# Two orders on ScalarE in a hybrid attention block: the mix gates' Sigmoids, and the first casts of the MLP's block sums

## The chip, the cores and the metric

One core of one Trainium2 chip. The metric is the device time of one execution in microseconds; the time of a kernel is the median of its runs. The engines are TensorE (PE; its weight loads are PEld), VectorE (DVE), ScalarE (ACT), GpSimd (POOL) and SyncE (SP, which here only issues DMAs).

## The reference

One layer with batch 1, sequence 1024, width 1024, all in float32. Cut to what matters:

```python
h = rms_norm(x, g_pre_mix)
proj = h @ w_in                       # q, k, v of both branches, and two gates of 1024 columns
gates = sigmoid(proj[..., c1:]);  gate_sb, gate_diff = split(gates, 2)
y_sb   = stick_breaking_attention(...)            # 8 heads of 64; sigmoids and a product along the keys
y_diff = differential_attention(...)              # 4 heads; two softmax maps, chunk-causal, T5 bias
y_diff = rms_norm(y_diff, w_subln) * (1 - lam_init)
merged = gate_sb * (y_sb @ w_sb_out) + gate_diff * (y_diff @ w_diff_out)
x = x + rms_norm(merged @ w_o, g_post_mix)
h = rms_norm(x, g_pre_mlp)
u = square(relu(h @ w_up))                        # 1024 -> 4096
x = x + rms_norm(u @ w_down, g_post_mlp)
```

## The kernel before

Every matrix product is made of three matmuls on split operands: an operand is cast to the matmul's type (`hi`, on ACT) and the rest is subtracted (`lo`, on DVE); the products are hi·hi, hi·lo and lo·hi. A cast followed by a subtraction is thus the commonest pair of instructions. Some of the gate projections and the whole MLP use a fast 2x2 block scheme with seven products in place of eight, on sums of blocks (T1 to T4 of the right operand, w1, w24, w32 of the left); the sums are formed on DVE or POOL.

The program is written in stages, and the Tile framework orders it (`schedule_with_timeline_sim=True`): it runs the whole program in a timing model and puts an instruction on its engine's list when the model has it ready, older work first. Each engine then works down its list in order, and waits at the head of it. The stages that matter here:

- *Attention* runs over eight units: four pairs of stick-breaking heads (`steps_sb`, Sigmoids on ACT), then four differential heads (`steps_diff`, Exps on ACT). A unit runs over four groups j of two query tiles in the order 3, 1, 2, 0. Its end, `finish_diff`, transposes the weights on PE (`tr_df`), splits them (`wth_df`, L298, and `wtl_df`), multiplies with v (`av_d`, L368 to L370), and for j = 1 and 0 normalises: a copy of `av_d` (L375), a Square, the split of it (`yp`, L379), a matmul with ones (`ss`, L382), then Ln (L385) and Exp (L386) on ACT, four DVE steps, and a split that is stored to DRAM as y. Between the steps of a unit the kernel fills PE with projections of the next unit and with gate products; beside the last unit these are `last_products` (L542 on PE: g_b, g_c, g_d; `split_pair` casts their weights at L596; page_v is a running sum).
- *One activation table at a time.* A manual dependency (`after`) keeps the differential Exps behind the last Sigmoid of the stick-breaking heads, and one table with both Ln and Exp is loaded there by hand. Any other table load is put in by the compiler ahead of an activation that the loaded table lacks.
- *The mix* follows. `load_gate` loads a gate from DRAM into a buffer that attention's score tiles also use (`big_s`, four of them), and takes the Sigmoid (L721). `half_mix` loads and splits a weight, calls `load_gate`, and makes a product of 24 matmuls (L755) from y into one of the four pairs of PSUM banks (acc, sc, tr, av). `merge` multiplies the banks with the gates (L766), adds the halves (L768) and splits the sum (L769, L770), which frees the banks and the gate buffers. Sixteen half products are made in all, two of them ahead.
- *The output projection* (`finish_tile`, L859) runs over eight row tiles, with norms; `store_h` transposes the MLP's input and stores it in blocks, and for the last two tiles copies it straight into `hraw`.
- *The MLP's entry*. `load_h` loads `hraw` back. Eight products (L981) of two pairs of weights are computed ahead with the blocks B11 and B21, which exist early; after B11 the bank is copied out (L1001, `p1s`), then B21 is added in the same bank and relu and square follow (L987, L988). Meanwhile DVE forms the block sums from `hraw` and `split` makes hi and lo of B22, T2, T1, T3 and T4 (L810 and L811), first for the 384 early columns, then for the last 128. Then `up_pair` runs over the sixteen pairs of weights.

Loads and most stores are issued by SP in list order.

Of the kernel before, what the change touches and what calls it, by code (L numbers as in the profile page):

```python
# [11 lines left out]
AF = mybir.ActivationFunctionType  # L12
# [30 lines left out]
def hybrid_block_kernel(  # L43
# [17 lines left out]
    nc = tc.nc  # L61
# [20 lines left out]
    def f32(ap):  # L82
        return ap.bitcast(F32)
# [71 lines left out]
    with ExitStack() as actx:  # L155
# [129 lines left out]
        def transposed(w, j, name):  # L285

            for g in range(j + 1):
                tr = tr_tile(f"tr_{name}_{g}")
                cols = [(2 * g, 0), (2 * g, 1)]
                cols += [(2 * g + 1, 0), (2 * g + 1, 1)] if g < j else [(2 * g + 1, 1)]  # L290
                for i, (kb, qi) in enumerate(cols):
                    nc.tensor.transpose(  # L292
                        tr[:, i * P:(i + 1) * P], w[qi][:, kb * P:(kb + 1) * P], ident
                    )
                n = len(cols) * P
                hi = pa.tile([P, HALF], F32R, tag="wt_hi", name=f"wth_{name}_{g}", bufs=2)
                lo = pa.tile([P, HALF], F32R, tag="wt_lo", name=f"wtl_{name}_{g}", bufs=2)
                nc.scalar.copy(hi[:, :n], tr[:, :n])  # L298
                nc.vector.tensor_tensor(lo[:, :n], tr[:, :n], f32(hi[:, :n]), op=ALU.subtract)  # L299
                yield 2 * g, slice(0, 256), hi[:, 0:256], lo[:, 0:256]  # L300
                if g < j:
                    yield 2 * g + 1, slice(0, 256), hi[:, 256:512], lo[:, 256:512]
                else:
                    yield 2 * g + 1, slice(P, 256), hi[:, 256:384], lo[:, 256:384]
# [4 lines left out]
        def pair_bank(key, j):  # L309

            if j > 1:
                banks[key, j % 2] = ps.tile([P, 2, 256], F32, tag="av", name=f"av_{key}_{j}", bufs=2)
            return banks[key, j % 2]

        def store_y(u, rows, j, yt):
            y_rows = y_dram[u][rows].rearrange("p l (h o c) -> p l h o c", h=2, o=2)
            for part in range(2):
                nc.sync.dma_start(out=y_rows[:, part, :, j % 2, :], in_=f32(yt[:, part]))
# [45 lines left out]
        def finish_diff(h, j, w, v):  # L364
            bank = pair_bank(f"d{h}", j)
            av = bank[:, j // 2, :]
            for kb, qc, hi, lo in transposed(w, j, f"df{h}_{j}"):
                nc.tensor.matmul(av[:, qc], v[:, kb, 0:P], hi, start=(kb == 0), stop=False)  # L368
                nc.tensor.matmul(av[:, qc], v[:, kb, 0:P], lo, start=False, stop=False)
                nc.tensor.matmul(av[:, qc], v[:, kb, P:2 * P], hi, start=False, stop=(kb == 2 * j + 1))  # L370
            if j > 1:
                return
            yt = pa.tile([P, 2, 256], F32, tag="part", name=f"y_{h}_{j}", bufs=2)
            sq, r = (pa.tile([P, 2, 256], F32, tag="small_s", name=f"{n}_{h}_{j}", bufs=4) for n in ("sq", "r"))
            nc.scalar.copy(yt, bank)  # L375

            nc.scalar.activation(sq, yt, AF.Square)
            both = pa.tile([P, 2, 2, 256], F32R, tag="yt", name=f"yp_{h}_{j}", bufs=1)
            nc.scalar.copy(both[:, 0], sq)  # L379
            nc.vector.tensor_tensor(both[:, 1], sq, f32(both[:, 0]), op=ALU.subtract)  # L380
            ss = ps.tile([P, 2, 256], F32, tag="av", name=f"ss_{h}_{j}", bufs=2)
            nc.tensor.matmul(ss, ones, both[:, 0], start=True, stop=False)  # L382
            nc.tensor.matmul(ss, ones, both[:, 1], start=False, stop=True)

            nc.scalar.activation(r, ss, AF.Ln, scale=1.0 / P, bias=eps_col)  # L385
            nc.scalar.activation(r, r, AF.Exp, scale=-0.5)  # L386
            nc.vector.scalar_tensor_tensor(sq, ss, P * EPS, r, op0=ALU.add, op1=ALU.mult)
            nc.vector.scalar_tensor_tensor(sq, sq, -0.5 / P, r, op0=ALU.mult, op1=ALU.mult)
            nc.vector.scalar_tensor_tensor(sq, sq, 1.5, r, op0=ALU.add, op1=ALU.mult)
            nc.vector.scalar_tensor_tensor(yt, yt, subln, sq, op0=ALU.mult, op1=ALU.mult)  # L390
            nc.scalar.copy(both[:, 0], yt)
            nc.vector.tensor_tensor(both[:, 1], yt, f32(both[:, 0]), op=ALU.subtract)
            store_y(N_SB + h, slice(0, P), j, both)

        def steps_diff(h, qs, kh, kl, v):
# [5 lines left out]
            for j in ORDER:  # L401
                w = []
                for qt in (2 * j, 2 * j + 1):
# [27 lines left out]
                    )  # L431
                    w.append(p1)
                yield 4 * j + 3, partial(finish_diff, h, j, w, v)

        last_sigmoid = [None]

        def after(ins, first):
            tc.add_manual_dep(
                ins.ins, first.ins.name,
                mybir.DependencyInfo(mybir.DependencyClass.NoSync, mybir.DependencyReason.DATA),  # L440
                reason="one activation table at a time",
            )
# [275 lines left out]
        def load_gate(b, i):  # L718
            g = pa.tile([P, S], F32, tag="big_s", name=f"g_{b}_{i}", bufs=4)
            nc.sync.dma_start(out=g, in_=gate_dram[i * NK + b])  # L720
            nc.scalar.activation(g, g, AF.Sigmoid)  # L721
            return g


# [68 lines left out]
    def pair_page(name, dt=F32R):  # L793
        return page(name, [P, 2, HALF], dt)
# [11 lines left out]
    def raw_tile(name, shape=None):  # L806
        return stream.tile(shape or [P, S], F32, tag="raw", name=f"raw_{name}")

    def split(hi, lo, raw):
        nc.scalar.copy(hi, raw)  # L810
        nc.vector.tensor_tensor(lo, raw, f32(hi), op=ALU.subtract)  # L811

    def bank(tag, name):
        return ps.tile([P, HALF], F32, tag=tag, name=name, bufs=2)
# [28 lines left out]
    def split_h(name, q, raw):  # L843
        split(*hb[name][q], raw)
# [106 lines left out]
    for t in range(NT):  # L951
# [12 lines left out]
        if t == 3:  # L964
            for name, j in (("B11", 0), ("B21", 1)):
                h_pages(name, big_pair)
                for q in range(2):
                    raw = raw_tile(f"h{name}{q}", [P, 2, HALF])
# [5 lines left out]
    def product(acc, a, b, first=True):  # L974

        a_hi, a_lo = a
        for k in range(4):
            ks = slice(k * P, (k + 1) * P)
            h_hi, h_lo = (x[:, k % 2, :] for x in hb[b][k // 2])
            for i, (st, mv) in enumerate(((a_hi, h_hi), (a_hi, h_lo), (a_lo, h_hi))):  # L980
                nc.tensor.matmul(  # L981
                    acc, st[:, ks], mv, start=(first and k == 0 and i == 0), stop=(k == 3 and i == 2),
                    skip_group_check=True,
                )

    def relu2(dst, src):
        nc.scalar.activation(dst, src, AF.Relu)  # L987
        nc.scalar.activation(dst, dst, AF.Square)  # L988

    def blocks(pages, i):  # L990
        return tuple(x[:, i * HALF:(i + 1) * HALF] for x in pages)
# [3 lines left out]
    p1s = [pair_page(f"p1_{i}", F32) for i in range(AHEAD // 2)]  # L995
    u11s = [pair_page(f"u11_{i}", F32) for i in range(AHEAD // 2)]
    for i in range(AHEAD // 2):
        accs = [bank(BANKS[i % 2], f"c11_{2 * i + e}") for e in range(2)]
        for e in range(2):
            product(accs[e], blocks(first_a[2 * i + e], 0), "B11")  # L1000
            nc.scalar.copy(p1s[i][:, e, :], accs[e])  # L1001
        for e in range(2):
            product(accs[e], blocks(first_a[2 * i + e], 1), "B21", first=False)
            relu2(u11s[i][:, e, :], accs[e])
            state.append((p1s[i][:, e, :], u11s[i][:, e, :]))
# [6 lines left out]
    for cs in (EARLY, LATE):  # L1012
        def split_part(name, q, raw):
            hi, lo = hb[name][q]
            split(hi[:, :, cs], lo[:, :, cs], raw)

        hs = [[hraw[j, c, q][:, :, cs] for j, c in ((0, 1), (0, 0), (1, 1), (1, 0))] for q in range(2)]
        for q, (b12, b11, b22, b21) in enumerate(hs):
            nc.vector.tensor_tensor(b11, b12, b11, op=ALU.subtract)
            split_part("B22", q, b22)  # L1020
            nc.vector.tensor_tensor(b12, b22, b12, op=ALU.subtract)
            nc.vector.tensor_tensor(b22, b22, b11, op=ALU.subtract)
            split_part("T2", q, b22)
        for q, (b12, b11, b22, b21) in enumerate(hs):
            split_part("T1", q, b11)
        for q, (b12, b11, b22, b21) in enumerate(hs):
            split_part("T3", q, b12)
        for q, (b12, b11, b22, b21) in enumerate(hs):
            nc.vector.tensor_tensor(b21, b21, b22, op=ALU.subtract)
            split_part("T4", q, b21)  # L1030
# [193 lines left out]
    for left, other in zip(STORED, ("B11", "T1", "T2", "T4", "T3", "B22", "B21")):  # L1224
        accs = [bank(BANKS[t], f"d{left}_{t}") for t in range(4)]
# [63 lines left out]
```

## Time and profile before

| what | value |
|---|---|
| median of 3 runs | 1462.94 us (1461.15 to 1464.65) |
| profiled execution | 1466.77 us |
| its span, first to last instruction | 1465.0 us |
| PE busy | 1432.6 us, 98% of the span |
| DVE, ACT, POOL busy | 1019.1, 759.3, 395.9 us |
| mean granted clock of PE | 0.995 |
| the 16 Sigmoids of L721 | 623.5 to 738.1 us from the start, 1.06 us each |
| the 8 Exps of L386 | 414.6 to 672.8 us |
| the 4 copies of L1001 | 844.1 to 863.0 us |

Rows of the profile are read so. In the order of time: start in us from the span's start, duration in us, engine, line of the kernel, operation, written tile <- read tiles, shape, and how many in a row; in brackets the idle time of the engine before it and what ended it (`<-DMA g<-gate_dram` is the DMA that wrote g). In the list of waits: who waited for whom, total us, times, longest. In a group: busy us, mean ns of one | idle us before them and what ended it. In a table by stretches: length, then busy us and count for each engine, then PE's granted clock, the share of the DMA engines and GB/s.

### The profile page before, as it was taken

How to read it: one execution, taken by the hardware profiler on the slowest of the kernel's cores; microseconds unless marked ns; L12 is line 12 of the kernel's file. 1: busy time of each engine (PE TensorE's matmuls, PEld its weight loads, DVE VectorE, ACT ScalarE, POOL GpSimd, SP SyncE). 2: the span in 40 equal slices, each digit the busy share in tenths (PEclk: the TensorE clock that was granted, in tenths of full speed). 3: DMA queues.
4: the chain of work that ended last, by engine and by line, in shares of the span. 5: the costliest groups of instructions: out<-in, count | busy, mean ns of one | idle time of the engine just before them, and what ended most of it. 6: DMA issues, size and time to landing. Idle time of an engine off the chain costs nothing.

```text
span 1465.0 us, 19999 instructions
## 1 busy us (share of the span) xinstructions
PE 1432.6 (98%) x7238; PEld 1213.6 (83%) x7238; DVE 1019.1 (70%) x1354; ACT 759.3 (52%) x1316; POOL 395.9 (27%) x393
## 2 busy tenths in 40 slices
PE   7999999999999999989999989999999999999997
PEld 6888998898889888768888877888888888888886
DVE  5477998898667768754756499766665669764783
ACT  5455666566566676464535364544444433534450
POOL 2012331244215002300002334333330257232611
PEclk9999999999999999999999999999999999999999
DMA  5432312222323256574657745544446785678681
GB/s 205 105 98 66 77 48 80 65 72 77 103 92 116 80 173 216 166 260 146 198 152 238 224 162 173 173 151 151 157 158 201 246 285 188 201 236 279 203 287 58
DMA packets 100283, 233.09 MB, mean 159 GB/s; under 512 B 9964, under 2 KB 25560, under 8 KB 100184
## 3 DMA queue, kind: packets, MB, share of 16 engines
q1 hardware_dynamic: 85784, 211.89, 45.1%
q10 hardware_dynamic: 14400, 19.93, 3.8%
q8 instruction: 57, 0.93, 0.3%
q14 instruction: 42, 0.34, 0.1%
HBM read 160.45 MB, written 65.29 MB: 154 GB/s over the span
## 4 chain that ended last, share of the span: by engine, by line
PE 87%; DVE 3%; issue 3%; DMA 2%; ACT 2%; POOL 1%; SPq 0%; POOLq 0%; ACTq 0%; DVEq 0%
PE dS L1157 12%; PE dA L1157 9%; PE mix L755 6%; PE o L859 5%; PE p_tr L981 5%; PE p_av L981 5%; PE c L981 5%; PE p_sc L981 3%; PE tr_sb L292 2%; PE z L274 2%; PE acc_gate L208 2%; PE acc_gate L206 2%; PE acc_gate L207 2%; PE z L273 2%; PE c L542 2%
## 5 line engine op out<-in xcount | busy, mean ns | idle before, releaser
L356 DVE TENSOR_TENSOR_SCAN rest<-rest 128x896 f32<-128x896 f32 (+3 forms) x64 | 88.1, 1385 | 16.3 <-POOL rest L351 15.6
L351 POOL TENSOR_SCALAR_AFFINE_SELECT rest<-rest 128x128 f32<-128x128 f32 x64 | 26.5, 414 | 242.3 <-ACT rest L347 237.6
L755 PE MATMUL mix<-y,wmix 128*128 128x512 f32 x384 | 88.0, 390 | 0.0
L755 PEld LDWEIGHTS mix<-y,wmix 128*128 128x128 f32 x384 | 71.9, 188 | 14.8
L811 DVE TENSOR_TENSOR lS_lo<-raw_S,lS_hi 128x1024 fp32r<-128x1024 f32 x32 | 52.2, 1630 | 39.5 <-ACT lS_hi L810 39.3
L1157 PE MATMUL dS<-rT_hi,lS_hi 128*128 128x512 f32 x192 | 74.7, 389 | 0.0
L1157 PE MATMUL dS<-rT_hi,lS_lo 128*128 128x512 f32 x192 | 74.7, 389 | 0.0
L1157 PE MATMUL dS<-rT_lo,lS_hi 128*128 128x512 f32 x192 | 74.7, 389 | 0.0
L810 ACT CAST lS_hi<-raw_S 128x1024 fp32r<-128x1024 f32 x32 | 33.7, 1052 | 74.3 <-DMA raw_S<-s_dramS 43.5
L419 ACT ACTIVATE s<-s,low 128x896 f32<-128x896 f32 (+7 forms) x64 | 49.7, 777 | 35.7 <-DVE low L414 35.6
L347 ACT ACTIVATE rest<-z 128x512 f32<-128x512 f32 (+2 forms) x96 | 47.9, 499 | 27.7 <-PE z L274 19.8
L426 POOL TENSOR_TENSOR sums<-sums,lam 128x1 f32<-128x1 f32 x32 | 8.8, 276 | 177.9 <-DVE sums L425 177.9
L981 PE MATMUL c<-hB_hi,wa_hi 128*128 128x512 f32 x128 | 50.8, 397 | 4.1 <-ACT p L1001 4.1
L299 DVE TENSOR_TENSOR wtl_sb<-tr_sb,wth_sb 128x512 fp32r<-128x512 f32 (+1 forms) x80 | 48.0, 628 | 8.5 <-ACT wth_sb L298 7.9
L298 ACT CAST wth_sb<-tr_sb 128x512 fp32r<-128x512 f32 (+1 forms) x80 | 41.2, 554 | 24.4 <-PE tr_sb L292 24.0
L351 POOL TENSOR_SCALAR_AFFINE_SELECT beta<-beta 128x128 f32<-128x128 f32 x64 | 52.4, 819 | 2.6 <-ACT beta L348 1.9
L207 PE MATMUL acc_gate<-h,hi_gate 128*128 128x512 f32 x128 | 50.6, 395 | 0.0
L208 PE MATMUL acc_gate<-h,lo_gate 128*128 128x512 f32 x128 | 50.5, 395 | 0.0
L206 PE MATMUL acc_gate<-h,hi_gate 128*128 128x512 f32 x128 | 50.4, 394 | 0.0
L981 PE MATMUL c<-hB_lo,wa_hi 128*128 128x512 f32 x128 | 50.4, 394 | 0.0
L981 PE MATMUL c<-hB_hi,wa_lo 128*128 128x512 f32 x128 | 50.1, 393 | 0.0
L1157 PE MATMUL dA<-rB_hi,lA_hi 128*128 128x512 f32 x128 | 49.8, 389 | 0.0
(400 smaller groups left out, 4867.2 us busy)
## 6 DMA issues: line engine op xcount, KB each, us to landing
s_dramS<-us SPq DMA_DIRECT2D x64, 256.0 KB, 3.7
raw_S<-s_dramS SPq DMA_DIRECT2D x32, 512.0 KB, 4.3
s_dramA<-u ACTq DMA_DIRECT2D x48, 256.0 KB, 3.3
raw_A<-s_dramA SPq DMA_DIRECT2D x24, 512.0 KB, 4.4
y<-y_dram SPq DMA_DIRECT2D x16, 512.0 KB, 5.5
g<-gate_dram SPq DMA_DIRECT2D x16, 512.0 KB, 4.0
raw_up<-in_w_up_dram SPq DMA_DIRECT2D x16, 512.0 KB, 4.0
up<-in_w_up_dram SPq DMA_DIRECT2D x16, 512.0 KB, 4.1
```

What stands on the lines that cost most here:

```text
L206: nc.tensor.matmul(acc, w_hi[:, ks], b_hi, start=(k == 0), stop=False)
L207: nc.tensor.matmul(acc, w_hi[:, ks], b_lo, start=False, stop=False)
L208: nc.tensor.matmul(acc, w_lo[:, ks], b_hi, start=False, stop=(k == NK - 1))
L299: nc.vector.tensor_tensor(lo[:, :n], tr[:, :n], f32(hi[:, :n]), op=ALU.subtract)
L351: nc.gpsimd.affine_select(tl[:, dg], tl[:, dg], pattern=[[-1, P]], compare_op=ALU.is_gt, fill=fill, base=0, channel_multiplier=1,)
L356: nc.vector.tensor_tensor_scan(back, back, back, 1.0, op0=ALU.mult, op1=ALU.bypass)
L419: e = nc.scalar.activation(s[:, :nk], s[:, :nk], AF.Exp, bias=low, scale=-1.0, accum_out=sums[:, m:m + 1],)
L755: nc.tensor.matmul(accs[c], st, mv[:, cs], start=(first and k == 0), stop=(last and k == 3))
L811: nc.vector.tensor_tensor(lo, raw, f32(hi), op=ALU.subtract)
L859: nc.tensor.matmul(accs[n], st, mv[:, n * HALF:(n + 1) * HALF], start=(first and k == 0), stop=(last and k == NK - 1),)
L981: nc.tensor.matmul(acc, st[:, ks], mv, start=(first and k == 0 and i == 0), stop=(k == 3 and i == 2), skip_group_check=True,)
L1157: nc.tensor.matmul(acc, st[:, e, ts], mv[:, e, :], start=(first and e == 0 and i == 0), stop=(last and e == 1 and i == 2))
```

## The change

Two dependencies that only order instructions on ACT; no instruction's work is changed. `finish_diff` keeps its last Exp in `last_exp`, and each Sigmoid of `load_gate` is put behind the one that is kept when the mix is written, the Exp of the last unit's group 0. At the MLP's entry the last of the copies of L1001 (`copied` is assigned anew at each of the four, so it holds the fourth) is put ahead of the four casts of T2. The other blocks' casts get no dependency, but stand behind those in program order.

```diff
-            nc.scalar.activation(r, r, AF.Exp, scale=-0.5)
+            last_exp[0] = nc.scalar.activation(r, r, AF.Exp, scale=-0.5)
...
-        last_sigmoid = [None]
+        last_sigmoid, last_exp = [None], [None]
...
             nc.sync.dma_start(out=g, in_=gate_dram[i * NK + b])
-            nc.scalar.activation(g, g, AF.Sigmoid)
+            after(nc.scalar.activation(g, g, AF.Sigmoid), last_exp[0])
...
-    def split(hi, lo, raw):
-        nc.scalar.copy(hi, raw)
+    def split(hi, lo, raw, behind=()):
+        cast = nc.scalar.copy(hi, raw)
+        for first in behind:
+            tc.add_manual_dep(
+                cast.ins, first.ins.name,
+                mybir.DependencyInfo(mybir.DependencyClass.NoSync, mybir.DependencyReason.DATA),
+                reason="evictions of the products ahead come first",
+            )
         nc.vector.tensor_tensor(lo, raw, f32(hi), op=ALU.subtract)
...
             product(accs[e], blocks(first_a[2 * i + e], 0), "B11")
-            nc.scalar.copy(p1s[i][:, e, :], accs[e])
+            copied = (nc.scalar.copy(p1s[i][:, e, :], accs[e]),)
...
-            split(hi[:, :, cs], lo[:, :, cs], raw)
+            split(hi[:, :, cs], lo[:, :, cs], raw, copied if name == "T2" else ())
```

## The prediction

> **What bounds the kernel now.** I read the page first: the busy shares, then the chain that ended last.
>
> ```profile
> PE 1432.6 (98%) x7238; PEld 1213.6 (83%) x7238; DVE 1019.1 (70%) x1354; ACT 759.3 (52%) x1316; POOL 395.9 (27%) x393
> ...
> PE 87%; DVE 3%; issue 3%; DMA 2%; ACT 2%; POOL 1%; SPq 0%; POOLq 0%; ACTq 0%; DVEq 0%
> ```
>
> TensorE (PE) bounds almost all of it. An edit that reorders ScalarE (ACT) can only pay where PE stands still or runs at a lower clock. So the second view is the waits of PE from 600 to 900 us, which hold both places of the change. In the same view from 900 us to the end there is no wait at all, so time won before 900 us is kept to the end, unless the new order makes a wait there.
>
> ```profile
> PE c L981 <- ACT p L1001: 4.1, 1, 4.1
> PE av_d L368 <- ACT wth_df L298: 3.8, 1, 3.8
> PE p L981 <- DVE hT_lo L811: 1.3, 2, 0.8
> PE g_d L542 <- DVE w_lo L597: 0.5, 1, 0.5
> ...
> PE ss L382 <- ACT yp L379: 0.5, 1, 0.5
> PE g_c L542 <- DVE page_v L624: 0.5, 1, 0.5
> ```
>
> The two largest waits are for ACT. The first edit is aimed at the second line, the second edit at the first. What stands in front of each on ACT decides, so I went to ACT's and PE's instructions in order of time.
>
> **Edit 1: the Sigmoids of the mix gates (L721) behind attention's last Exp (L386).** First ACT's groups from 600 to 760 us, the table loads among them; then rows of ACT and of PE in order of time.
>
> ```profile
> L721 ACT ACT_TABLE_LOAD x4 | 5.1, 1283 | 5.4 <-DMA g<-gate_dram 5.3
> L419 ACT ACT_TABLE_LOAD x2 | 2.6, 1283 | 0.0
> L385 ACT ACT_TABLE_LOAD x2 | 2.6, 1283 | 0.0
> L386 ACT ACT_TABLE_LOAD x2 | 2.6, 1283 | 0.0
> ```
>
> ```profile
> 622.23 1.28 ACT L721 ACT_TABLE_LOAD   x1 [2.52 <-DMA g<-gate_dram]
> ...
> 632.90 1.28 ACT L419 ACT_TABLE_LOAD   x1
> ...
> 634.98 1.03 ACT L596 CAST w_hi<-fw 128x1024 fp32r<-128x1024 f32 x1
> 638.84 1.28 ACT L721 ACT_TABLE_LOAD   x1 [2.82 <-DMA g<-gate_dram]
> 640.13 1.06 ACT L721 ACTIVATE g<-g 128x1024 f32<-128x1024 f32 x1
> 641.21 1.28 ACT L386 ACT_TABLE_LOAD   x1
> 642.50 0.63 ACT L386 ACTIVATE r<-r 128x512 f32<-128x512 f32 x1
> 643.04 1.06 ACT L298 CAST wth_df<-tr_df 128x512 fp32r<-128x512 f32 x2
> ...
> 643.66 0.38 PE L368 MATMUL av_d<-wth_df,v_dfv 128*128 128x256 f32 x1 [3.76 <-ACT wth_df L298]
> 644.51 4.60 PE L542 MATMUL g_c<-T,page_w 128*128 128x512 f32 x12 [0.47 <-DVE page_v L624]
> ```
>
> ACT works in order. A Sigmoid stands at its head and waits for its gate's DMA, loads its table and runs; the Exp behind it loads another table; only then come the casts that PE waits for. With the Sigmoids gone from this stretch, ACT is free at 634.98 + 1.03 = 636.0. The Exp (0.63) and the two casts (1.06) follow and end at about 637.7, while PE has work until 643.66 - 3.76 = 639.9. The 3.76 us vanish with 2.2 us to spare. The vector engine (DVE) waited for the same Exp before page_v, so the 0.47 goes too. The wait for yp (0.5) has the Sigmoid of 622.23 ahead of it, which cost ACT 2.52 + 1.28 + 1.06. The wait for w_lo (0.5) comes after the weight cast at 634.98, which has the load of 632.90 ahead of it, 1.28 us that go; late next there could be the weight's buffer, which an earlier product must free, and if it is, that half microsecond stays. Sum of the four: 3.76 + 0.47 + 0.5 + 0.5 = 5.2 us.
>
> Behind the long wait PE runs slowly: the last row has twelve matmuls in 4.60 us, one every 0.38. In the mix (quoted below) 132 of the same size take 30.08, one every 0.23, which makes 2.9 for twelve. The 1.7 us more go with the wait. The granted clock bears it out: 0.87 between 644 and 657 us.
>
> ```profile
> 620.00:644.00 24.00, 19.21 (x95) 15.17 (x93) 9.07 (x19) 18.78 (x26) 4.74 (x6) 1.00 0.52 170
> 644.00:657.00 13.00, 12.53 (x60) 10.48 (x59) 9.27 (x20) 4.15 (x11) 0.19 (x1) 0.87 1.02 381
> ```
>
> (Columns: stretch, us, then busy us of PE, PE's weight loads, DVE, ACT, POOL, then clock, DMA share, GB/s.) PE idles 24.00 - 19.21 + 13.00 - 12.53 = 5.26 us here, the same 5.2. Edit 1 is worth 5.2 + 1.7 = 6.9 us when nothing takes its place; its floor is 0 if another wait does.
>
> Nine of the ten table loads should go, 9 x 1.283 = 11.5 us of ACT; that is no time of PE's beyond what is counted.
>
> If a wait stays in this place but a shorter one, is the slow clock still paid? The rows have only long ones (3.8, 4.1) with it. [...]
>
> What must hold for the 6.9 us to last is the start of the mix, where the Sigmoids now land.
>
> ```profile
> 657.03 5.26 PE L755 MATMUL mix<-y,wmix 128*128 128x512 f32 x22
> ...
> 670.12 30.08 PE L755 MATMUL mix<-y,wmix 128*128 128x512 f32 x132
> ...
> 657.03:670.12 13.09, 12.59 (x52) 9.72 (x53) 1.00 0.63 210
> ...
> L766 DVE TENSOR_TENSOR g<-mix,g 128x512 f32<-128x512 f32 x32 | 20.8, 686 | 27.7 <-PE mix L755 21.3 <-ACT g L721 6.4
> ...
> 670.32 0.69 ACT L385 ACTIVATE r<-ss,eps_col 128x512 f32<-128x512 f32 x1 [1.98 <-PE ss L383]
> ...
> 672.83 0.63 ACT L386 ACTIVATE r<-r 128x512 f32<-128x512 f32 x1
> ...
> 637.73 11.73 SPq L734 DMA_DIRECT2D y<-y_dram  x9
> ```
>
> The mix then starts 6.9 earlier, at 650.1. The last Exp comes 6.9 and one table load (1.28) earlier, at 664.7. The first Sigmoid ends at 664.7 + 0.63 + 1.28 + 1.06 = 667.6, and two multiplications on DVE (0.69 each) free its banks at 669.0. PE has four half products of 24 matmuls for its four pairs of banks, less the six that need the last head: 90 x 0.23 = 20.7. To that comes the last head's own work between them, 13.09 - 52 x 0.23 = 1.1 us by the row of L755 alone. So it wants banks back at 650.1 + 20.7 + 1.1 = 672. That leaves 3 us. Queued behind the Sigmoids on ACT are the weight casts of the mix and the cast of the last head's output. That cast waits for four DVE steps after the Exp, longer than the load and two Sigmoids, and the saved load covers one more. The gate loads on SP's queue are issued where they are now: what SP waits for is a free buffer, and the Sigmoid does not set that. The y loads (nine in 11.73 us) share full DMA engines; with three issued before, the fifth of the nine completes heads 0 to 3 (two loads a head), is issued near 643.4, and is wanted at 650.1 + 18 x 0.23 = 654. I cost these at nothing; their bound is 3 us of the gain if the covers are gone.
>
> **Edit 2: the four casts of T2 (L810 by way of the split) behind the fourth copy of a product (L1001).** ACT, PE and DVE in turn:
>
> ```profile
> 851.93 0.84 ACT L810 CAST hT_hi<-hraw 128x768 fp32r<-128x768 f32 x1 [5.12 <-DVE hraw L1022]
> ...
> 860.58 0.83 ACT L810 CAST hT_hi<-hraw 128x768 fp32r<-128x768 f32 x1 [3.88 <-DVE hraw L1022]
> ...
> 862.97 0.59 ACT L1001 COPY p<-c 128x512 f32<-128x512 f32 x1 [0.40 <-ACT u L988]
> ...
> 863.61 0.80 PE L981 MATMUL c<-hB_hi,wa_hi 128*128 128x512 f32 x1 [4.07 <-ACT p L1001]
> ...
> 883.10 0.50 PE L981 MATMUL p<-hT_lo,w_hi 128*128 128x512 f32 x1 [0.79 <-DVE hT_lo L811]
> ...
> 860.00:884.00 24.00, 19.08 (x75) 15.02 (x76) 22.74 (x32) 17.09 (x29) 5.90 (x4) 0.93 0.26 88
> ```
>
> PE stopped at 863.61 - 4.07 = 859.54. The product that the copy reads ended one product (twelve matmuls, 2.7 us) before that, near 856.8. ACT stood idle then, at the head of its queue a T2 cast waiting for DVE until 860.58. With the copy first, it ends near 857.4, inside ACT's idle 3.88 us, and PE goes on at 859.54 without the 4.07. As above, PE runs slowly behind such a wait (0.93 of the clock in this stretch); I take 1.4 us for it, most of the 1.7 measured above, so PE arrives 5.5 us earlier at the first product with T2.
>
> But the next thing late is DVE. It is busy for 22.74 of the 24.00 us after 860, and the wait at 883.10 is for its last hT_lo. PE's work before that point would be done sooner, and would wait longer for the same DVE. Only DVE's own gaps, 24.00 - 22.74 = 1.26 us, can move 883.10. On the other side, the first T2 cast moves from 851.93 to past 857, and its DVE subtraction with it; if nothing fills that place DVE loses about 0.9. If, instead, the planner finds PE other products to do meanwhile, up to the whole 5.5 is won. The bounds are -0.9 and +5.5; I take +1.0, because DVE's row is the one that ends last.
>
> One row bears on how much DVE's work there costs:
>
> ```profile
> 853.68 2.04 DVE L811 TENSOR_TENSOR hB_lo<-hraw,hB_hi 128x768 fp32r<-128x768 f32 x1
> ...
> 861.14 0.95 DVE L1029 TENSOR_TENSOR hraw<-hraw,hraw 128x768 f32<-128x768 f32 x1
> ...
> 852.99 1.91 POOL L935 TENSOR_TENSOR s<-up 128x512 f32<-128x512 f32 x1 [7.31 <-DVE hraw L1029]
> ```
>
> The same size takes 2.04 us while POOL works and 0.95 when it does not, and POOL forms four sums of weights for every pair of products here. If T2's subtractions, moved later, fall on POOL's work, each of up to four costs DVE 1.1 us more, 4.4 in all; this stands under the rivals. [...]
>
> **Sum.** 6.9 + 1.0 = 7.9 us. The profiled execution took 1466.77 us (span 1465.0 and 1.77 around it), so 1458.9 by it. It lies 3.8 above the median of the runs, 1462.94; against that median the forecast is 1455.0.
>
> **The rivals.**
> 1. *Edit 2 pays in full*, because PE's order is made anew and products of the next pair fill the wait: 1462.9 - 6.9 - 5.5 = 1450.5. For it: the listed order already mixes products. Against it: these need weight halves that DVE must subtract too. 12%.
> 2. *A new wait takes about half of edit 1*, or edit 2 costs DVE some us: the banks of the mix come late by up to the 3 us margin and more, or T2 held back 5 us (851.93 to 857) leaves DVE idle or meets POOL's sums (4.4). With 3 to 6 us lost: 1458 to 1461. 20%.
> 3. *No change.* The order is made by a simulated run of the whole program; the planner puts other ACT work, such as the mix's weight casts, before the casts PE wants, and PE waits as before: about 1463. 6%.
> 4. *Slower.* The last head's matmuls (av_d, ss) are placed behind more of the mix than now. Then every Sigmoid is behind that Exp, all banks stay full, and PE has nothing to do. It decides from where the banks come free over 7.9 + 2.9 = 10.8 us after PE wants them: at 683 instead of my 669, the Exp 14 us later than I put it, at 679. At 5 us beyond that point the time is 1471. Against it: the planner gives the attention's older work priority, as at 662 to 670. 7%.
>
> **How the numbers follow.** My forecast holds 55%: 1452.5 to 1459. What a measurement can tell from no change is 0.2%, 2.9 us. Faster by more: 55 + 12 + 13 of rival 2 = 80%; within: 7 of rival 2 and 6 of rival 3 = 13%; slower: 7%. The range runs from rival 1 with a microsecond to spare, 1449.5, to the end of rival 2, 1461; about 15% lies outside.
>
> **What would show it.** Right, edit 1: one ACT table load between 600 and 760 us where there are ten; the wait of av_d for wth_df gone; no wait of PE for L755 between 650 and 700; the first mix matmul at about 650. Right, edit 2: the wait for p gone, the fourth copy near 850 (857 less the 7 won earlier), and in its place a longer wait of a product for hT_lo. Wrong: a wait of PE in the mix for g's multiplication; the last Exp later against the mix's start than 15.8 us; DVE idle at the MLP's entry for a cast of T2; or any PE wait after 900 us, which the order before does not have.

## The result and the profile after

| kernel | median | runs | ratio to before, 95% interval |
|---|---|---|---|
| before | 1462.94 us (1460.55 to 1471.22) | 9 | 1 |
| after | 1455.49 us (1453.29 to 1461.11) | 9 | 0.9948 (0.9934 to 0.9963) |

The forecast was 1455.0 us. The median fell by 7.45 us, which by the interval is 5.4 to 9.7. The profiled execution took 1458.88 us, 3.4 above its median, so it may not be set against the median of before; its span is 1457.1.

First the page of the changed kernel: busy time of the engines, then the chain that ended last by engine.

```profile
PE 1430.6 (98%) x7238; PEld 1213.3 (83%) x7238; DVE 1018.1 (70%) x1354; ACT 748.3 (51%) x1307; POOL 392.8 (27%) x393
...
PE 88%; DVE 3%; DMA 3%; issue 2%; ACT 2%; POOL 1%; SPq 0%; DVEq 0%; POOLq 0%; ACTq 0%
```

ACT has nine instructions less (1307 for 1316), which are nine table loads, and 11.0 us less work. PE still carries the chain. Next, PE's waits from 600 to 900 us; from there to the end there is again none. All lines after L810 or so are six higher than before (L1001 is now L1007, L981 is L987).

```profile
PE p_sc L987 <- DVE w_lo L817: 1.8, 1, 1.8
PE mix L755 <- DMA y<-y_dram: 1.2, 1, 1.2
PE trh L891 <- DVE or L883: 0.8, 1, 0.8
PE p L987 <- DVE hT_lo L817: 0.5, 1, 0.5
```

Both waits for ACT are gone. New are 1.8 us for DVE's w_lo at the MLP's entry, and 1.2 us for a y tile in the mix. The wait for hT_lo, which the prediction expected to grow, is 0.5 where it was 1.3. The stretches that were shown of before:

```profile
620.00:644.00 24.00, 24.00 (x129) 20.58 (x128) 17.01 (x38) 13.41 (x27) 5.70 (x7) 1.00 0.73 230
644.00:657.00 13.00, 13.00 (x66) 10.89 (x65) 3.74 (x6) 3.20 (x6) 0.00 (x0) 1.00 1.03 388
```

PE, the first busy column, has no gap left between 620 and 657, where it had 5.26 us of them, and the clock is 1.00 where it was 0.87. Now the start of the mix in order of time, PE, then ACT, DVE and SP's queue:

```profile
650.56 1.52 PE L755 MATMUL mix<-y,wmix 128*128 128x512 f32 x6
...
662.65 17.16 PE L755 MATMUL mix<-y,wmix 128*128 128x512 f32 x75
680.98 39.28 PE L755 MATMUL mix<-y,wmix 128*128 128x512 f32 x172 [1.17 <-DMA y<-y_dram]
...
664.28 0.62 ACT L745 CAST wmix<-raw_mix 128x512 fp32r<-128x512 f32 x1 [5.29 <-DMA raw_mix<-in_w_mix_dram]
664.80 0.68 ACT L385 ACTIVATE r<-ss,eps_col 128x512 f32<-128x512 f32 x1
665.52 0.63 ACT L386 ACTIVATE r<-r 128x512 f32<-128x512 f32 x1
666.17 1.28 ACT L721 ACT_TABLE_LOAD   x1
667.46 3.90 ACT L721 ACTIVATE g<-g 128x1024 f32<-128x1024 f32 x4
...
668.55 1.29 DVE L766 TENSOR_TENSOR g<-mix,g 128x512 f32<-128x512 f32 x2 [0.95 <-ACT g L721]
...
674.13 0.38 SPq L318 DMA_DIRECT2D y_dram<-yp  x1
```

The mix starts at 650.56, with one table load and four Sigmoids behind the last Exp. The first banks are multiplied out by 668.55 + 1.29 = 669.8, and PE does not stop for a bank. It stops 1.17 us for y, until 680.98. That is the last head's y, which goes by way of DRAM: its second store is issued at 674.13.

To follow PE through the whole program I subtracted the start of each matmul of one trace from that of the same matmul in the first trace of before, and took the median over a stretch. Negative is earlier. After against before: +1.7 us near 605 (the order is still the same there, so this is the execution, not the change), -6.6 at 672, -5.1 at 700, -4.6 at 852, -7.8 from 885 to the end. So 8.3 us are won up to the mix, 1.5 given back at the wait for y, and 3.2 won at the entry. The rest, 0.5, is lost on the way from the mix to the entry.

### The profile page after: what moved, and what is told of

Read it like the earlier page. It is cut to its first block, busy times and chain, and to the rows that moved or that the text cites. A ratio compares the mean times of both kernels' runs of the same rounds, so it can differ in the third digit from the quotient of the medians.

```text
span 1457.1 us, 19996 instructions
## 1 busy us (share of the span) xinstructions
PE 1430.6 (98%) x7238; PEld 1213.3 (83%) x7238; DVE 1018.1 (70%) x1354; ACT 748.3 (51%) x1307; POOL 392.8 (27%) x393
## 4 chain that ended last, share of the span: by engine, by line
PE 88%; DVE 3%; DMA 3%; issue 2%; ACT 2%; POOL 1%; SPq 0%; DVEq 0%; POOLq 0%; ACTq 0%
PE dS L1163 12%; PE dA L1163 9%; PE o L865 6%; PE c L987 5%; PE p_av L987 5%; PE p_tr L987 5%; PE mix L755 4%; PE p_sc L987 3%; PE z L274 2%; PE tr_sb L292 2%; PE z L273 2%; PE acc_gate L207 2%; PE acc_gate L206 2%; PE acc_gate L208 2%; PE c L542 2%
## 5 line engine op out<-in xcount | busy, mean ns | idle before, releaser
L810 ACT CAST lS_hi<-raw_S 128x1024 fp32r<-128x1024 f32 x32 | 33.6, 1051 | 74.2 <-DMA raw_S<-s_dramS 43.4
L817 DVE TENSOR_TENSOR lA_lo<-raw_A,lA_hi 128x1024 fp32r<-128x1024 f32 x24 | 36.5, 1522 | 20.3 <-ACT lA_hi L810 18.8
L987 PE MATMUL c<-hB_lo,wa_hi 128*128 128x512 f32 x128 | 49.9, 390 | 0.0
L987 PE MATMUL c<-hB_hi,wa_hi 128*128 128x512 f32 x128 | 49.9, 390 | 0.0
```

What stands on the lines that cost most here:

```text
L987: nc.tensor.matmul(acc, st[:, ks], mv, start=(first and k == 0 and i == 0), stop=(k == 3 and i == 2), skip_group_check=True,)
```

## Experiments

Two numbers are used for each trace, both by that subtraction: the *tail*, from 605 to 700 us, where edit 1 acts, and the *entry*, from 852 to 885, where edit 2 acts.

**Each edit by itself.** Edit 1 alone leaves out `copied` and `behind`; edit 2 alone leaves out the dependency of the Sigmoids.

```diff
 # edit 1 alone, against after
-            copied = (nc.scalar.copy(p1s[i][:, e, :], accs[e]),)
+            nc.scalar.copy(p1s[i][:, e, :], accs[e])
 # edit 2 alone, against after
-            after(nc.scalar.activation(g, g, AF.Sigmoid), last_exp[0])
+            nc.scalar.activation(g, g, AF.Sigmoid)
```

> The first edit alone; the MLP's entry as before. Theory (the two edits add, each in its own place): attention's tail gains about 8 us up to the first mix matmul, about 1.5 us are given back at a wait for the last head's y, net 6 to 7 us faster: 1456 to 1457 against 1462.9. At the MLP's entry the 4 us wait of PE for the fourth copy is back. Rival (the edits only pay together, because DVE at the entry would take back what PE won before): less than 3 us faster.

> The second edit alone; Sigmoids as before. Theory (DVE is the bound at the MLP's entry, and the edit pays by moving DVE's work out of POOL's way): 2 to 3.5 us faster, 1459.5 to 1461, though the wait of PE that is removed with its slow clock is 5.5 us. Rival A (the removed wait of PE is what pays): 5 us or more faster, 1458 or less. Rival B (DVE ends at the same time whatever PE does): within 1 us of before.

Edit 1 alone: 1458.51 us (12 runs) against 1463.01 for before, ratio 0.9967 (0.9951 to 0.9982). Edit 2 alone: 1461.15 (12 runs), ratio 0.9981 (0.9967 to 0.9994). The product of the two ratios is 0.9948, which is what both together measured: as far as these intervals can tell, the edits add. Edit 1 is worth 4.5 us by the medians and 4.8 by the ratio, edit 2 1.9 and 2.8. The second is more than the 1.0 that I gave it, the first less than the 6.9, though both of my terms lie inside the intervals (2.6 to 7.2 and 0.9 to 4.8 us).

The traces give 8.2 us in the tail for edit 1, with no wait for y. The surprise is the entry: with edit 1 alone, its order of casts as before, it came out 3.8 us shorter too.

**POOL's sums at the entry left out**, with the order of before and with edit 2. Two pairs of weights then lack their block sums (one block is loaded by DMA in their place), so only the times are read.

```diff
         a11, a12, a21, a22 = (f[:, i * HALF:(i + 1) * HALF] for f in (f0, f1) for i in range(2))
+        if n in (1, 2):
+            nc.sync.dma_start(out=s1, in_=w_up[2 * n][:, 0:HALF])
+            return n, wa, s1, f0, f1
         nc.gpsimd.tensor_tensor(s1, a21, a22, op=ALU.add)
```

> The kernel before, with POOL's four sums left out for the second and the third pair of weights of the MLP (s1 is loaded by a DMA instead, the other blocks stay as loaded; the output differs). One look, for the stretch of DVE at the MLP's entry. Theory (POOL blocks DVE): the eight DVE instructions that took 1.1 us more than their size there take their normal time, so the stretch from the second L1019 to the last hT_lo shrinks by about 8.7 us, from 35.9 to 27, less what waits appear. Rival (those instructions are slow for another reason, such as DMA traffic): 35 us as before.

> The second edit alone, with the same sums of POOL left out (the output differs). To be held against the run before it. Theory (the second edit pays because POOL's sums now meet a DVE that idles): with POOL quiet in both, the second edit gains nothing or loses up to 1 us at the MLP's entry, for DVE idles some 2 us for the first T2 cast. Rival (it pays through PE's wait): it still gains 2.5 us or more there.

1453.35 and 1459.05 us, one run each; the difference between them lies in the tail, where the waits for ACT were 1.3 and 4.0 us, not at the entry. What counts is the entry: 7.3 us shorter than before with the old order, 6.9 with edit 2. With POOL quiet edit 2 is worth nothing, rather -0.4, by one trace of each. DVE's table over its work at the entry, from its third subtraction of 768 columns to the end of the last hT_lo (columns: stretch, length, busy us of DVE, PE's clock, DMA share, GB/s), for before, then for these two:

```profile
847.13:883.04 35.91, 34.62 (x41) 0.95 0.31 112
```

```profile
840.67:867.09 26.42, 25.75 (x41) 1.00 0.49 174
```

```profile
846.36:874.20 27.84, 25.06 (x40) 1.00 0.45 162
```

The same 41 instructions take DVE 34.62 us beside POOL and 25.75 without it. The order after edit 2 has DVE idle 2.78 us (27.84 - 25.06) where the old one has 0.67.

**Before and after once more, and two attempts to take the new wait for y away**: the Sigmoids behind the last cast of y (L391) instead of the last Exp; then also the weight cast that stood in front of the last Ln put behind the Exp.

```diff
 # behind the cast of y
-            nc.scalar.copy(both[:, 0], yt)
+            last_exp[0] = nc.scalar.copy(both[:, 0], yt)
 # the weight cast too (the Sigmoids then wait for last_cast, the copy above)
-            nc.scalar.copy(w[:, 0, :], raw)
+            cast = nc.scalar.copy(w[:, 0, :], raw)
+            if (b, i) == (1, 1):
+                after(cast, last_exp[0])
```

> The kernel before once more, for its profile. The wait of av_d for wth_df was 3.8 us in the first profile and 3.3, 1.3 and 4.0 in three runs that leave that stretch alone. Theory (the wait is set by when the gate's DMA lands, and differs between executions, so the first edit is worth less on average than the first profile says): again between 0 and 4 us, with slow matmuls behind it only where it is over about 3. Rival (the wait is fixed by the order of the work): 3.8 again, and the MLP's entry lasts as long as in the first profile within 1 us.

> The changed kernel once more, timed beside the next two. By both theories 0.995 of before; its profile shows whether the wait of the mix for y (1.2 us in the first profile, none in the run with the first edit alone) is there in this execution.

> The changed kernel with the Sigmoids put behind the cast of the last head's output (L391) and not behind its Exp. Theory (the last head's y comes late because the table load, four Sigmoids and the gates' multiplications stand ahead of its last steps): y is stored some 3 us earlier, the wait for y in the mix is gone, 0 to 1.2 us faster than the changed kernel. Rival (then the banks come free too late, with the first multiplication near 672): a wait of PE in the mix of 0.5 to 2 us instead, no faster or slower by up to 2 us.

> The same, and the weight cast that stood ahead of the last Ln and waited 5.3 us for its DMA (b = 1, i = 1) is put behind the Exp. Theory: the Ln runs as soon as PE has the sum, some 1.9 us earlier; y and the banks both come in time, no wait of PE in the mix, 0.5 to 1.5 us faster than the changed kernel. Rival (the y wait is rare and small): within 0.7 us of the changed kernel.

Before gave 1468.41 in its traced run, with waits of 3.5 and 4.7 us for ACT. After: 1455.04 us (8 runs), 0.9954 (0.9938 to 0.9971). Behind the cast of y: 1455.91 (12 runs), 0.9959 (0.9945 to 0.9973). The weight cast too: 1454.88 (8 runs), 0.9951 (0.9933 to 0.9968). The three can't be told apart. In the first variant the wait for y is gone, but PE waits 0.6 us for g's multiplication instead; in the second both are there.

```profile
PE mix L755 <- DVE g L766: 0.6, 1, 0.6
```

```profile
PE mix L757 <- DMA y<-y_dram: 0.7, 1, 0.7
PE mix L757 <- DVE g L768: 0.6, 1, 0.6
```

So moving the Sigmoids further back wins nothing that can be measured: PE is within about 1 us of both its banks and its y there, and when the one wait goes the other comes.

**More traces of the entry in its old order.** Edit 1 alone twice more, before once more.

> Edit 1 alone once more, for a second trace of the MLP's entry in the order of before. Theory: with the casts of T2 in their old place the entry is unsteady, because DVE's wait for the fourth copy and POOL's two sets of sums meet in another way in each execution; the first trace of this order was a lucky one (3.8 us shorter than before). So the wait of PE for the fourth copy is 3 us or more here, the entry takes about what it took in the first two traces of before, within 2 us of them, and the time is about 1458 us. Rival: edit 1 itself shortens the entry, because everything arrives 7 us earlier; then the entry is 3 to 4 us shorter than before again and the time about 1452 us.

> The same as the run before it, a third trace. Theory: a long wait for the fourth copy (3 us or more) in at least one of the two. Rival: under 1 us in both, and an entry 3 to 4 us shorter than before in both. At the mix both expect what edit 1 showed so far: no wait for its split weights, the mix's start 8 us earlier than in the profile of before at equal time ahead of it.

> The kernel before, a third trace. Theory: the wait of the last head's product for its split weights is one of 3 to 4 us, and the entry is unsteady: its length from the first to the last of DVE's subtractions differs from the first two traces by more than the 0.5 us by which those with edit 2 differ among each other. Rival: it is as steady as with edit 2, and edit 2 takes a fixed time out of it.

1460.26, 1458.63 and 1463.72 us, one run each; a further run of before beside them took 1465.89. The short entry of the first trace of edit 1 was one outcome of an unsteady order: the next two are 1.0 and 1.7 us longer than the first trace of before. The third trace of before is 3.1 shorter. The expected long wait for the fourth copy is there in one of the two (4.4); in the other PE waited 3.4 us for a weight's cast instead. All traces in which POOL forms the sums, in the order of DVE's stretch:

| order at the entry | trace | DVE's stretch, us | of it idle | blocked by POOL | entry against before |
|---|---|---|---|---|---|
| old | before, third | 31.3 | 0.7 | 4.9 | -3.1 |
| old | edit 1 alone, first | 31.3 | 0.7 | 4.9 | -3.8 |
| old | before, first | 35.9 | 1.3 | 8.7 | 0 |
| old | edit 1 alone, third | 37.2 | 2.6 | 8.7 | +1.7 |
| old | before, second | 37.3 | 2.7 | 8.7 | +2.0 |
| old | edit 1 alone, second | 37.6 | 3.0 | 8.7 | +1.0 |
| edit 2 | the weight cast too | 33.0 | 0.9 | 7.0 | -4.0 |
| edit 2 | after, second | 33.2 | 0.1 | 8.1 | -2.8 |
| edit 2 | edit 2 alone | 33.5 | 0.6 | 7.8 | -3.5 |
| edit 2 | after, first | 33.6 | 2.4 | 6.1 | -3.2 |
| edit 2 | behind the cast of y | 33.7 | 1.6 | 7.0 | -3.4 |

("Blocked" is the sum by which DVE's two-input instructions last longer than the same size alone: 0.955, 0.685 and 0.415 us for 768, 512 and 256 columns.) The old order takes 31.3 or 36 to 37.6, the new one 33.0 to 33.7 each time. The mean of the entry is -0.35 in the old order and -3.4 in the new, so edit 2 is worth 3.0 us by the traces, and 1.9 to 2.8 by its own experiment. It wins this by taking away the long outcome, which four of the six traces of the old order have; against the two short ones it wins nothing. How often the untraced runs have the long outcome is not known.

What decides in the old order is seen when a short and a long trace are put side by side: DVE's nine hT_lo and the first of POOL's second set of sums. First the third trace of before, then the third of edit 1 alone.

```profile
870.87 5.76 DVE L811 TENSOR_TENSOR hT_lo<-hraw,hT_hi 128x768 fp32r<-128x768 f32 x9
...
874.74 3.04 POOL L935 TENSOR_TENSOR s<-raw_up 128x512 f32<-128x512 f32 x1 [14.49 <-DMA raw_up<-in_w_up_dram]
```

```profile
861.11 1.29 DVE L811 TENSOR_TENSOR hT_lo<-hraw,hT_hi 128x768 fp32r<-128x768 f32 x2 [1.08 <-ACT hT_hi L810]
863.24 0.69 DVE L1048 TENSOR_TENSOR v<-p_sc,p 128x512 f32<-128x512 f32 x1 [0.84 <-PE p_sc L981]
863.85 10.15 DVE L811 TENSOR_TENSOR hT_lo<-hraw,hT_hi 128x768 fp32r<-128x768 f32 x9
...
865.35 1.81 POOL L935 TENSOR_TENSOR s<-raw_up 128x512 f32<-128x512 f32 x1 [14.98 <-PE p L981]
```

POOL's second set starts 28.0 and 27.6 us after the stretch begins (846.78 and 837.76); in the six traces of the old order it is 27.6 to 28.3. In the short one DVE reached its nine instructions at 24.1 us and was two thirds through when POOL came; there it was POOL's sum that was held up (3.04 us for the usual 1.3). In the long one it had idled for hT_hi (1.08) and for p_sc (0.84), reached them at 26.1, and met all four sums: 10.15 us for what took 5.76. Two microseconds of idle time of DVE became six. In the first trace of before 0.6 us more of idle time than in the short ones was enough: POOL's second set came first there too, and the stretch is 4.6 us longer.

**The sums on DVE.** If DVE is the bound of the entry and POOL's sums only get in its way, it should form them itself.

```diff
+        eng = nc.vector if n in (1, 2) else nc.gpsimd
-        nc.gpsimd.tensor_tensor(s1, a21, a22, op=ALU.add)
+        eng.tensor_tensor(s1, a21, a22, op=ALU.add)
...            # the three subtractions likewise
```

> Both edits, and the two sets of four sums that POOL forms at the MLP's entry are formed on DVE instead; nothing else changes. Theory (what bounds the entry is DVE, and POOL's sums block it for about as long as they run): each set costs DVE four additions of 0.68 us, 2.7 in all, and takes away the 3.5 to 4.4 us by which its own instructions are too long beside POOL's. DVE's stretch, from its third subtraction of 768 columns to the last hT_lo, becomes 25.1 + 2 x 2.7 = 30.5 us or shorter (27.8 if the second set is placed behind the last hT_lo) against 33.0 to 33.7 in the five traces with edit 2, and no instruction in it is longer than alone; the time falls by 2 to 4 us, to 1452 to 1453.5. Rival: POOL's time there is free and DVE's is not, so the eight additions lengthen the entry by up to 5.4 us: 1458 to 1461. A second rival: in DVE's list the additions wait for the weights' DMA and hold up the subtractions behind them; then DVE idles for the DMA in the trace, and the time is no better than 1455.

1452.16 us (1449.90 to 1453.70, 6 runs), ratio 0.9923 (0.9904 to 0.9941): the best kernel of this study. The seventeen runs of after lie between 1453.29 and 1461.11; the interval of this ratio overlaps theirs at its edge (0.9934 to 0.9941), so the 3 us are likely rather than certain. DVE's table over the same work, and PE's waits from 600 to 900:

```profile
839.45:869.57 30.12, 28.15 (x45) 1.00 0.37 134
```

```profile
PE p_sc L988 <- DVE w_lo L817: 1.2, 1, 1.2
PE mix L755 <- DMA y<-y_dram: 0.8, 1, 0.8
PE trh L891 <- DVE or L883: 0.3, 1, 0.3
```

DVE has five instructions more in the stretch (three of the eight additions come behind it) and is 3 us faster than after; none of them lasts longer than alone. The entry is 5.9 us shorter than before, against 3.4 on average in the five traces of edit 2 above. DVE does idle once for the weight's DMA in this trace (1.77 us), as the second rival has it, but the gain is larger than that.

## Why the prediction was right, and which steps were not

*Total: right.* 1455.0 against 1455.49 and 1455.04 in two jobs.

*Edit 1, the mechanism: right.* One table load instead of ten; the waits for wth_df, page_v, yp and w_lo gone; the mix at 650.56 for the predicted 650.1; the first two multiplications done at 669.8 for the predicted 669.0. The three traces of edit 1 alone have the tail 8.0 to 8.2 us shorter than the first trace of before. The six traces without edit 1 show how far that depends on one execution: their wait for wth_df was 3.8, 3.5, 3.7, 3.3, 4.0 and, once, 1.3 us. On average over these six, the tail is 7.7 us shorter with edit 1 alone (three traces), and 6.6 in the five traces with both edits or a variant of them, where the wait for y or for g takes some back. The 6.9 stands, then, as a reading of the traces; the timed runs of edit 1 alone say 4.5 (2.6 to 7.2). Why they say less is open. The mean granted clock of those runs is 0.9969, and 0.9960 in the runs of before beside them; 0.0009 of 1460 us is an estimate of 1.3 us for the slow clock, near the 1.7 of the sum, so by it the shortfall lies rather in the waits, sized at 5.2. One of the three traces also gave time back outside the tail and the entry: the second waits 1.5 us for ACT's ht at 788 and loses 2.0 us from 700 to 852. The three traced executions of before (1466.77, 1468.41, 1463.72) all lie above its medians (1462.3 to 1463.0), so their traces may overstate the wait; no trace of a run at the median is there to show it.

*The slow clock behind the wait: right.* With the wait of 1.3 us (POOL's sums left out, old order) the twelve matmuls behind it took 3.01 us, 0.25 each, at a granted clock of 1.00 (640.32 to 646 us); with 4.0 us, 5.49, at a mean clock of 0.62 from 644 to 650.

```profile
639.47 0.38 PE L368 MATMUL av_d<-wth_df,v_dfv 128*128 128x256 f32 x1 [1.30 <-ACT wth_df L298]
640.32 3.01 PE L542 MATMUL g_c<-T,page_w 128*128 128x512 f32 x12 [0.47 <-DVE page_v L624]
```

```profile
642.31 0.58 PE L368 MATMUL av_d<-wth_df,v_dfv 128*128 128x256 f32 x1 [4.00 <-ACT wth_df L298]
643.16 5.49 PE L542 MATMUL g_c<-T,page_w 128*128 128x512 f32 x12 [0.27 <-DVE page_v L624]
```

*What must hold for it to last: nearly right.* The banks came in time. The y loads, costed at nothing, cost 1.5 and 1.2 us in the two traces of after. I had looked at the loads of heads 0 to 3 only; the late one is the last head's, which has to go through DRAM after four DVE steps, and DVE puts gate multiplications between them. That is rival 2's mechanism at less than half the size that it had there.

*Edit 2: the term was mis-sized, 1.0 for about 3.0 by the traces and 1.9 to 2.8 by the timed runs (whose interval, 0.9 to 4.8, only just includes 1.0).* That DVE is late next was right, and the full 5.5 of rival 1 never came: with edit 2 alone PE still waits 3.3 us at the entry.

```profile
PE p_sc L987 <- DVE w_lo L817: 1.3, 1, 1.3
PE p L987 <- DVE hT_lo L817: 1.0, 1, 1.0
PE p_tr L987 <- DVE hT_lo L817: 1.0, 1, 1.0
```

The step that failed is "only DVE's own gaps, 1.26 us, can move 883.10". It took DVE's busy time as fixed work. But 8.7 of the 34.62 busy us were time blocked by POOL, and without POOL's sums the same work took 25.75. Against the four long traces of the old order, DVE's stretch with edit 2 is 3.6 us shorter on average: 1.5 less blocked, 1.3 less idle, and 0.7 for an operation on u that now follows the last hT_lo. In the trace of edit 2 alone the last hT_lo ends 3.27 us earlier than before (879.77 for 883.04): 0.88 because the stretch began earlier, 0.70 less idle, 0.95 less blocked, and 0.7 for the operation on u (41 instructions become 40). The risk that the prediction named came out otherwise: I feared that T2's subtractions, moved later, would meet POOL's sums. What they do is leave DVE waiting for a T2 cast behind the fourth copy while POOL runs its first set, so the two losses cover each other: in the table the trace with 0.1 us idle has 8.1 blocked, the one with 2.4 idle has 6.1, and the length is the same. The rows of after, DVE and then POOL:

```profile
850.02 1.40 DVE L1035 TENSOR_TENSOR hraw<-hraw,hraw 128x256 f32<-128x256 f32 x1
853.61 2.59 DVE L817 TENSOR_TENSOR hT_lo<-hraw,hT_hi 128x768 fp32r<-128x768 f32 x2 [2.19 <-ACT hT_hi L810]
...
854.02 1.90 POOL L944 TENSOR_TENSOR up<-up 128x512 f32<-128x512 f32 x1
```

I had named this idle time as a sign of failure; beside POOL it is free. The prediction had the row that shows the cause, 2.04 us beside POOL for 0.95; I used it as a risk for moved instructions, and not on those that stood in the stretch already.

*Two errors against each other.* By the medians of the timed runs edit 1 gave less than its term and edit 2 more, and the sum came out. That it came out within half a microsecond is luck; the total alone would not have shown it.

## What to carry to other kernels

Split an engine's busy time into work and blocked time before calling it a floor: compare each size's duration beside POOL with that alone. Where a bound engine shares its time with a helper, ask whether it would do the helper's work faster itself: here eight additions of 0.68 us, 5.5 in all, replaced 6.1 to 8.1 us of blocking. And take the waits of several executions before pricing an order: a wait that hangs on when a DMA lands was 1.3 to 4.0 us long in six traces in which that stretch has the same order (ACT stood 0.35 us for the gate's DMA in the shortest, 3.07 in the longest).

## What the runs showed of the hardware

Where DVE and POOL both worked, their instructions lasted longer than alone. In the first trace of before they ended in turn, one of each: POOL's first four sums at 854.90, 856.88, 858.31 and 859.73, four of DVE's instructions at 855.72, 857.16, 858.58 and 860.55. POOL's lasted 1.35 to 1.91 us for 1.29. DVE's lasted 2.04 for 768 columns (0.95 alone) and 1.50 and 1.52 for 256 (0.41 alone); in after one of 256 columns lasted 1.40 (the row above). The price was 1.0 to 1.1 us in these five, whatever the size, so the small ones paid most for their length: 1.40 is 3.4 times 0.41, and 2.04 is 2.1 times 0.95.

The slow clock did not need a wait as long as those of before. In the trace of after it followed a wait of 1.84 us: the granted clock is 0.50 from 861.50 to 864.91, with matmuls of 0.63 us for 0.39 from 861.79 on. In the first trace of edit 1 alone a wait of 2.29 us was followed by none. The stretch with most of the wait and the two behind it look so, first after, then edit 1 alone (columns: stretch, length, PE's busy us, the clock, the DMA share and GB/s):

```profile
856.00:860.00 4.00, 2.56 (x12) 1.00 0.17 66
860.00:864.00 4.00, 3.60 (x11) 0.69 0.62 190
864.00:868.00 4.00, 4.00 (x17) 0.89 0.39 137
```

```profile
852.00:856.00 4.00, 1.67 (x7) 1.00 0.01 4
856.00:860.00 4.00, 4.00 (x18) 1.00 0.85 244
860.00:864.00 4.00, 4.00 (x20) 1.00 0.39 145
```

So the length of a wait alone does not say here whether the clock falls. Nor does it in the first trace of before: the clock is 0.50 from 593.74 to 597.15, from 644.94 to 648.35 and from 863.39 to 866.80, and PE's longest waits at these three were 0.99, 3.76 and 4.07 us. What else decides is open.
